# A kernel that plans its own instruction order: two prices of its planner and the size of four copies are changed

## The chip, the cores and the metric

The kernel runs on one core of one Trainium2 chip. The core has TensorE (PE in the profile, PEld for its weight loads), VectorE (DVE), ScalarE (ACT), GpSimd (POOL) and a queue for transfers (SP). The metric is the time of one execution on the device, in microseconds (us). Less is better.

## The reference

The reference runs three blocks over 256 tokens of width 1024, all in float32. It has six feed-forward networks around three token mixers: a short convolution, a gated delta rule, and a pair of sparse attention and an RWKV-7 scan. Cut to the part that matters here, the gated delta rule (16 value heads, 8 key heads of width 128) is:

```
a = strict_lower(einsum(k_beta, k) * decay)       # one key matrix per head and chunk
t_inv = solve(eye + a, eye)                       # its triangular inverse
u, w = t_inv @ v_beta, t_inv @ (k_beta * exp(g))
out = ... @ w_out                                 # after the state recurrence over chunks
```

Before it stands a projection `x @ w_in` that gives q, k, v, z and the gates, with a causal convolution of four taps over q, k and v.

## The kernel before

All weight matrices are cut into 128x128 tiles, four tiles to a chunk of 256 KB, and streamed from HBM in the order of use. A float32 product is made of three matmuls in the fast 32-bit format ("streamed products" below): each chunk `wraw` is split by ScalarE into `whi` (a copy) and by VectorE into `wlo` (the rest), the activations likewise into `xh` and `xl`, and TensorE multiplies whi by xh, whi by xl and wlo by xh, 256 columns each, into a bank of PSUM. Seven split chunks can be held ahead.

While the projection of the gated delta rule streams, the work of the mixer is done beside it: 256-column results are taken from the banks, the convolution taps of a v column (`conv`, three scalar_tensor_tensor on VectorE) read the bank itself, so the bank is free only when its last tap is done; from the eleventh column on, this product has three banks in turn, two columns to a bank (the line `banks=lambda g: 7 if g < 3 else 3`).

Beside it runs the chain `side`: the key matrices `TT` of 16 heads and two chunks of 128 tokens are inverted. `to_blocks` gathers their 32x32 diagonal blocks with copies on ScalarE and turns them with one VectorE transpose of 128x1024. `invert_blocks` then does 62 dependent VectorE instructions (31 steps of a product and a subtraction), `from_blocks` two more such transposes, and `inverse` goes from 32x32 to 128x128 by small matmuls. All that follows (values, states, outputs, and so the projection `gdn_out` behind it) waits for that inverse. The RWKV mixer later uses the same functions for 16 matrices.

The order of instructions on each engine is not that of the program text. Every instruction is recorded as a node with a price in us (`Pace.price`) and its dependences. `Pace.ranks` lays all nodes out by list scheduling over the five engines, forward and backward in five rounds (`Pace.schedule`), keeps the shortest plan, and `Pace.arrange` fixes each engine's order as the plan has it. So a price never changes how long an instruction takes; it changes the order in which engines take their instructions. An engine that is free in the plan takes the node of the highest priority that is ready. The chain `side` is put back by 3 us in priority (`SIDE = -3.0`). The prices also move the clocks by which the parts of the program are interwoven when it is written down (`weave`) and by which chunks are split ahead (`split_ahead`). The plan ends an instruction before it takes the next: a ScalarE copy holds ScalarE for its whole price.

Of the kernel before, what the change touches and what calls it, by code (L numbers as in the profile page):

```python
# [12 lines left out]
F32R = mybir.dt.float32r  # L13
U32 = mybir.dt.uint32
AF = mybir.ActivationFunctionType
# [244 lines left out]
class Pace:  # L260
# [43 lines left out]
    def price(self, engine, op, out, ins, kw):  # L304
        n = 1
        for d in (ins[0] if op == "tensor_reduce" else out).shape[1:]:
            n *= d
        if engine == "tensor":
            return self.columns(op, out, ins)[0] / 2400 + 0.0025
        held = 0.06 if hasattr(kw.get("scale"), "tensor") or hasattr(kw.get("bias"), "tensor") else 0.0  # L310
        bank = ins and self.parts(ins[0])[0][0].startswith("bank")
        if engine == "scalar":
            return (0.05 if bank else 0.09) + n * 0.00084 + 1.5 * held + (0.09 if "accum_out" in kw else 0.0)
        if engine == "gpsimd":
            return 0.1 + n * 0.002
        if op in ("tensor_copy", "tensor_scalar", "memset"):
            return 0.07 + n * (0.00104 if bank else 0.0006)
        if op == "reciprocal":
            return 0.07 + n * 0.00625
        return (0.13 if op == "scalar_tensor_tensor" else 0.07) + n * 0.00104  # L320

    def columns(self, op, out, ins):
# [42 lines left out]
    def schedule(self, order, before, after, forward):  # L365
# [16 lines left out]
        while left:  # L382
# [10 lines left out]
            else:  # L393
                t, e = min((free[e] if now[e] else max(free[e], later[e][0][0]), e) for e in free if now[e] or later[e])
                while later[e] and later[e][0][0] <= t:
                    _, o, i = heapq.heappop(later[e])
                    heapq.heappush(now[e], (o, i))
                o, i = now[e][0]
                _, price, _, cols = self.nodes[i]
                if e in self.LOOK and forward and later[e]:  # L400
                    w = min((c for c, u, j in later[e] if j in self.urgent and i not in self.urgent and c - t < self.WAIT * price), default=None)
                    if w is not None:
                        free[e] = max(w, t + 1e-6)
                        heapq.heappush(later[e], (free[e], *heapq.heappop(now[e])))
                        while now[e]:
                            heapq.heappush(later[e], (free[e], *heapq.heappop(now[e])))
                        continue
                if e == "tensor" and forward and len(now[e]) > 1 and cols[1] < 1500 * price:
                    while recent and recent[0][0] < t + price - self.TICK:
                        count -= recent.popleft()[1]  # L410
                    heavy = count + cols[1] < self.AIM + (self.MORE if heavy else 0)
                    if heavy:
                        o, i = min(((o, i) for o, i in now[e] if self.nodes[i][3][1] >= 2000 * self.nodes[i][1]), default=(o, i))
                        _, price, _, cols = self.nodes[i]
# [283 lines left out]
class Kernel:  # L698
# [769 lines left out]
    def to_blocks(self, TT, compact, blk):  # L1468

        M = TT.shape[1]  # L1470
        d = compact.rearrange("p (m i) -> p m i", i=32)
        for q in range(4):
            s = slice(32 * q, 32 * q + 32)
            self.nc.scalar.activation(d[s], TT[s, :, s], AF.Copy)
        d = d.rearrange("p m i -> p i m")
        if M == 16:
            d = d[:, :, None, :].to_broadcast([P, 32, 2, 16])
        self.nc.vector.transpose(blk.rearrange("p (j i) -> p i j", i=32), d)
# [745 lines left out]
```

## Time and profile before

| | |
|---|---|
| median of the runs shown | 1549.7 us (1548.59 to 1553.14, 3 runs) |
| the profiled execution | 1541.02 us |
| its span, first to last instruction | 1538.8 us |
| mean granted TensorE clock | 0.994 |

The profiled execution took 1541.02 us, of which 1538.8 us lie between its first and last instruction; 2.2 us lie around it. It is 0.56% below the median of the runs, so a change worked out in the profile is carried over by the ratio. Times in the trace count from the first instruction. All instructions are issued by one helper line, so the trace is read by tiles and not by lines.

### The profile page before, as it was taken

How to read it: one execution, taken by the hardware profiler on the slowest of the kernel's cores; microseconds unless marked ns; L12 is line 12 of the kernel's file. 1: busy time of each engine (PE TensorE's matmuls, PEld its weight loads, DVE VectorE, ACT ScalarE, POOL GpSimd, SP SyncE). 2: the span in 40 equal slices, each digit the busy share in tenths (PEclk: the TensorE clock that was granted, in tenths of full speed). 3: DMA queues.
4: the chain of work that ended last, by engine and by line, in shares of the span. 5: the costliest groups of instructions: out<-in, count | busy, mean ns of one | idle time of the engine just before them, and what ended most of it. 6: DMA issues, size and time to landing. Idle time of an engine off the chain costs nothing.

```text
span 1538.8 us, 35927 instructions
## 1 busy us (share of the span) xinstructions
PE 1522.6 (99%) x13544; PEld 1473.0 (96%) x13544; DVE 1197.5 (78%) x2527; ACT 1024.2 (67%) x2153; POOL 10.4 (1%) x24
## 2 busy tenths in 40 slices
PE   9999999999999999999999999999999999999999
PEld 9999999999999999989898899999997877999999
DVE  7776597887659777689997768775888866889984
ACT  7556566765657557678797866565783666578863
POOL 0000000000000000000000000000001000000000
PEclk9999999999999999999999999999999999999999
DMA  8766666566665667525343357666533313566674
GB/s 280 200 194 194 184 187 195 168 202 194 194 196 174 196 195 248 184 83 172 117 125 104 105 164 210 195 192 194 172 116 123 103 58 87 171 190 198 194 201 129
DMA packets 142670, 261.14 MB, mean 170 GB/s; under 512 B 15904, under 2 KB 17952, under 8 KB 142368
## 3 DMA queue, kind: packets, MB, share of 16 engines
q1 hardware_dynamic: 142496, 258.84, 56.8%
q8 instruction: 106, 1.74, 0.5%
q14 instruction: 68, 0.56, 0.1%
HBM read 257.73 MB, written 1.05 MB: 168 GB/s over the span
## 4 chain that ended last, share of the span: by engine, by line
PE 94%; DVE 3%; ACT 2%; issue 1%; DMA 0%; SPq 0%; DVEq 0%; ACTq 0%
PE bank L576 94%; DVE a L576 1%; DVE wlo L576 1%; ACT a L576 1%; DMA wraw<-wstream 0%; DVE arG L576 0%; ACT stm L576 0%; DVE stm L576 0%; ACT arG L576 0%; ACT whi L576 0%; DVE fg L576 0%; DVE xl L576 0%; DVE pad L576 0%; DVE tmp L576 0%; ACT pad L576 0%
## 5 line engine op out<-in xcount | busy, mean ns | idle before, releaser
L576 ACT ACTIVATE whi<-wraw 128x512 fp32r<-128x512 f32 x956 | 599.0, 630 | 398.7 <-PE bank L576 199.7
L576 DVE TENSOR_TENSOR wlo<-wraw,whi 128x512 fp32r<-128x512 f32 x956 | 652.4, 688 | 257.5 <-ACT whi L576 252.0
L576 PE MATMUL bank<-xh,whi 128*128 128x256 f32 x2688 | 745.4, 281 | 6.1 <-DVE stm L576 3.6
L576 PE MATMUL bank<-xh,wlo 128*128 128x256 f32 x2688 | 743.8, 281 | 0.0
L576 PE MATMUL bank<-xl,whi 128*128 128x256 f32 x2688 | 737.8, 279 | 0.7 <-DVE xl L576 0.7
L576 PEld LDWEIGHTS bank<-xh,whi 128*128 128x128 f32 x2688 | 503.0, 189 | 14.8 <-issue 5.6
L576 PEld LDWEIGHTS bank<-xl,whi 128*128 128x128 f32 x2688 | 501.4, 188 | 8.1 <-issue 6.2
L576 PEld LDWEIGHTS bank<-xh,wlo 128*128 128x128 f32 x2688 | 501.5, 188 | 6.6 <-issue 5.6
L576 PE MATMUL bank<-a,whi 128*128 128x256 f32 x2272 | 389.0, 277 | 0.3
L576 PEld LDWEIGHTS bank<-a,whi 128*128 128x128 f32 x2272 | 342.4, 188 | 1.3 <-DVE a L576 0.5
L576 PE MATMUL bank<-a,wlo 128*128 128x256 f32 x1136 | 313.8, 276 | 0.0
L576 PEld LDWEIGHTS bank<-a,wlo 128*128 128x128 f32 x1136 | 213.3, 188 | 0.0
L576 DVE TENSOR_TENSOR tmp<-bank,rb 128x256 f32<-128x256 f32 x176 | 66.2, 417 | 5.4 <-ACT rb L576 1.0
L576 ACT ACTIVATE xh<-h,par 128x256 fp32r<-128x256 f32 x70 | 34.1, 500 | 12.3 <-DVE h L576 10.8
L576 ACT ACTIVATE a<-tmp 128x256 fp32r<-128x256 f32 x88 | 35.6, 405 | 8.7 <-DVE tmp L576 8.7
L576 ACT ACTIVATE arG<-bank 128x256 f32<-128x256 f32 (+2 forms) x87 | 37.8, 443 | 4.9 <-PE bank L576 4.7
L576 DVE TENSOR_TENSOR acc<-acc,tmp 128x256 f32<-128x256 f32 x92 | 38.5, 418 | 2.0 <-ACT acc L576 0.9
L576 DVE SCALAR_TENSOR_TENSOR arG<-arG,par 128x256 f32<-128x256 f32 x88 | 40.0, 478 | 0.0
L576 DVE TENSOR_TENSOR a<-tmp,a 128x256 fp32r<-128x256 f32 x88 | 36.7, 417 | 3.8 <-ACT a L576 3.8
L576 PE MATMUL bank<-a 64*128 64x256 f32 (+3 forms) x192 | 38.1, 372 | 1.5 <-DVE arG L576 1.5
L576 ACT ACTIVATE tmp<-tmp 128x256 f32<-128x256 f32 x88 | 35.3, 406 | 3.8 <-DVE tmp L576 3.7
L576 DVE TENSOR_TENSOR tmp<-tmp,tmp 128x256 f32<-128x256 f32 x88 | 36.6, 416 | 0.0
(253 smaller groups left out, 1226.1 us busy)
## 6 DMA issues: line engine op xcount, KB each, us to landing
wraw<-wstream SPq DMA_DIRECT2D x968, 256.0 KB, 2.9
arG<-cmp_w SPq DMA_DIRECT2D x1, 1024.0 KB, 4.7
out_dram<-h SPq DMA_DIRECT2D x8, 128.0 KB, 3.0
con<-consts SPq DMA_DIRECT2D x1, 734.0 KB, 5.8
h<-xt SPq DMA_DIRECT2D x1, 512.0 KB, 6.3
a<-lowrank SPq DMA_DIRECT2D x1, 512.0 KB, 3.7
par<-params SPq DMA_DIRECT2D x1, 283.5 KB, 4.8
h<-xt SPq DMA_DIRECT2D x2, 128.0 KB, 3.6
```

What stands on the lines that cost most here:

```text
L576: i = f(*args, **kw)
```

## The change

Three edits. A streamed product of n columns is priced n/2259 us in place of n/2400 + 0.0025 (for 256 columns 113.3 ns in place of 109.2 ns). A VectorE transpose gets a price of its own, 0.07 + n x 0.00184 us in place of 0.07 + n x 0.00104 (for 1024 elements 1.95 us in place of 1.13 us). In `to_blocks`, each copy of diagonal blocks is done 16 matrices at a time: for the 32 matrices of the gated delta rule, eight copies of 32x512 elements in place of four of 32x1024; for the 16 of the RWKV mixer nothing changes.

```
-            return self.columns(op, out, ins)[0] / 2400 + 0.0025
+            n = self.columns(op, out, ins)[0]
+            return n / 2259 if ins[0].dtype == F32R else n / 2400 + 0.0025
...
-        if op == "reciprocal":
-            return 0.07 + n * 0.00625
+        if op in ("reciprocal", "transpose"):
+            return 0.07 + n * (0.00625 if op == "reciprocal" else 0.00184)
...
-            self.nc.scalar.activation(d[s], TT[s, :, s], AF.Copy)
+            for m in range(0, M, 16):
+                self.nc.scalar.activation(d[s, m:m + 16], TT[s, m:m + 16, s], AF.Copy)
```

## Rows read from the trace of the kernel before

**Rows 1.** The page: span, and each engine's busy time, share, instructions.

```profile
span 1538.8 us, 35927 instructions
...
PE 1522.6 (99%) x13544; PEld 1473.0 (96%) x13544; DVE 1197.5 (78%) x2527; ACT 1024.2 (67%) x2153; POOL 10.4 (1%) x24
```

**Rows 2.** Windows: stretch, length, busy us per engine, granted clock, DMA share, GB/s.

```profile
755.00:759.30 4.30, 4.30 (x40) 4.30 (x39) 2.56 (x6) 4.24 (x6) 0.00 (x0) 1.00 0.82 237
759.30:763.10 3.80, 0.22 (x2) 0.04 (x2) 3.80 (x10) 3.77 (x6) 0.00 (x0) 0.91 0.02 8
763.10:770.00 6.90, 6.89 (x31) 6.67 (x32) 5.99 (x18) 4.43 (x11) 0.00 (x0) 0.55 0.39 118
770.00:812.00 42.00, 41.78 (x426) 41.22 (x426) 39.97 (x104) 36.63 (x77) 0.00 (x0) 1.00 0.44 132
812.00:856.00 44.00, 42.16 (x582) 37.97 (x576) 29.35 (x59) 33.72 (x90) 0.00 (x0) 0.96 0.23 73
...
1100.00:1310.00 210.00, 205.99 (x1882) 171.23 (x1881) 167.89 (x401) 141.11 (x339) 9.08 (x18) 0.98 0.33 101
```

**Rows 3.** Waits from 750 to 775 us: who waited for whom, total, times, longest.

```profile
PEld bank L576 <- ACT acc L576: 3.8, 1, 3.8
...
DVE a L576 <- ACT a L576: 1.7, 1, 1.7
```

**Rows 4.** Timeline around that wait: start, length, engine, instruction, idle before it.

```profile
754.46 4.26 ACT L576 ACTIVATE a<-a 32x1024 f32<-32x1024 f32 x4
...
758.74 0.47 ACT L576 ACTIVATE tmp<-bank,par 128x256 f32<-128x256 f32 x1
758.75 2.12 DVE L576 STREAM_TRANSPOSE a<-a 128x1024 f32<-128x1024 f32 x1 [1.74 <-ACT a L576]
...
760.76 0.45 DVE L576 SCALAR_TENSOR_TENSOR tmp<-bank,par,tmp 128x255 f32<-128x255 f32 x1
...
762.09 0.87 DVE L576 SCALAR_TENSOR_TENSOR tmp<-bank,par,tmp 128x254 f32<-128x254 f32 x2
...
763.08 0.29 PEld L576 LDWEIGHTS bank<-xh,whi 128*128 128x128 f32 x1 [3.76 <-ACT acc L576]
```

**Rows 5.** Windows of a quiet streaming stretch, PE alone: busy us, matmuls, clock.

```profile
80.00:120.00 40.00, 40.00 (x355) 1.00 0.68 193
```

**Rows 6.** The page's DMA issues: the weight stream.

```profile
wraw<-wstream SPq DMA_DIRECT2D x968, 256.0 KB, 2.9
```

**Rows 7.** Groups by shape: count, busy us, mean ns, idle before.

```profile
L576 DVE STREAM_TRANSPOSE a<-a 128x1024 f32<-128x1024 f32 x6 | 12.6, 2116 | 4.4 <-ACT a L576 4.4
...
L576 ACT ACTIVATE a<-a 32x512 f32<-32x512 f32 x8 | 4.9, 626 | 0.1
L576 ACT ACTIVATE a<-a 32x1024 f32<-32x1024 f32 x4 | 4.2, 1055 | 0.0
```

**Rows 8.** Windows, only PE instructions that read xh: busy us, count, clock.

```profile
810.00:820.00 10.00, 3.98 (x16) 0.83 0.40 134
820.00:830.00 10.00, 3.11 (x18) 1.00 0.15 36
830.00:840.00 10.00, 2.27 (x9) 1.00 0.47 151
```

**Rows 9.** Timeline of VectorE: chunk splits and transposes back to back.

```profile
808.52 3.94 DVE L576 STREAM_TRANSPOSE a<-a 128x1024 f32<-128x1024 f32 x2
...
814.14 1.88 DVE L576 TENSOR_TENSOR wlo<-wraw,whi 128x512 fp32r<-128x512 f32 x3
```

**Rows 10.** Windows of ten us in the RWKV mixer, columns as in the second group.

```profile
1110.00:1120.00 10.00, 8.59 (x76) 8.40 (x75) 9.98 (x22) 8.60 (x18) 0.00 (x0) 1.00 0.75 242
...
1170.00:1180.00 10.00, 8.53 (x38) 6.14 (x38) 9.47 (x19) 1.22 (x3) 0.71 (x1) 0.83 0.17 52
...
1240.00:1250.00 10.00, 10.00 (x188) 8.08 (x189) 5.49 (x14) 9.08 (x21) 0.00 (x0) 0.83 0.39 129
```

## The prediction

> **What bounds the kernel now.** I read the page first. TensorE is busy for 1522.6 of 1538.8 us, no other engine for more than 78% [rows 1]. So only three things can change the time: the 16.2 us in which TensorE does nothing, the stretches in which its clock is low, and its work, which this change leaves alone. About 2 us of the idle time lie at the start and 3 at the end, which no order removes. Next the windows by stage: a quiet streaming stretch has no idle time at all [rows 5]; the idle time lies beside the two large mixers [rows 2]. Then the waits: the largest of TensorE in the gated delta rule is one of 3.8 us [rows 3]. The timeline shows where: at 763.08 us a weight load starts after 3.76 us of idling [rows 4]. Behind the wait the granted clock is 0.55 for 6.9 us [rows 2]. With only the levels 1.2 and 2.4 GHz, a mean of 0.55 is 90% of the stretch, 6.2 us, at 1.2 GHz, and half of that, 3.1 us, is lost. The place costs 3.8 + 3.1 = 6.9 us.
>
> What is late there? The waits name ScalarE's `acc`, but the load is the first of a new column, which needs a bank, and a bank is free when the last tap has read it: the two taps from 762.09 last 0.87 us and end at 762.96, 0.12 us ahead of the load [rows 4]. The taps are late because VectorE stood idle for 1.74 us for the block copies and then transposed for 2.12 us; ScalarE spent 4.26 us on four copies in a row, and the activation that starts the taps' column waited behind them until 758.74 [rows 4]. So this one wait lies just where all three edits act.
>
> **The change part by part.** No instruction's own duration changes but those of the copies. The rest is order.
>
> *Transposes.* Six, 2.12 us each in the mean, 1.97 back to back [rows 7, 9]. The price goes from 1.13 to 1.95, so the planner sees 0.82 us more for each and can put taps or splits first. Direct cost nothing.
>
> Here the Trainium skill speaks against the edit: its Vector Engine (DVE) Microarchitecture Reference, section "The reshape front-end and per-opcode configuration", says a transpose is pipelined to sustain one element per cycle per lane, an estimate of 1.07 us for 1024 elements at the 0.96 GHz that its page VectorE: DVE Perf Modes gives. By it the old price would be right and the edit worth nothing; the trace disagrees with twice that, 1.97 us.
>
> *Copies.* Four of 1055 ns become eight of 626 ns [rows 7]: 5.01 - 4.22 = 0.79 us more on ScalarE. It is busy in 36.63 of the 42 us from 770 on [rows 2], so this has room, but not in the 4.3 us ahead of the transpose, where ScalarE is 4.24 us busy [rows 2]. The gain is that ScalarE can take another instruction every 0.6 us instead of every 1.05: the tap's activation and two splits stood behind the copies. What is queued behind a copy on ScalarE is thus less delayed; what waits for all eight copies (the transpose, the chain) comes up to 0.79 us later, more if splits go between.
>
> *Streamed products.* 968 chunks of four tiles [rows 6] with three matmuls each are 11,616; each is planned 4.1 ns longer, 48 us in all. The quiet stretch gives 40 us / 355 = 112.7 ns [rows 5]; the old price is 3.2% short, the new 0.5% long. In the old plan TensorE needs its splits and banks earlier than it really does.
>
> The Trainium skill's page TensorE: Matmul & The Clock Gate, section "Wait — 56ns, not 53.3ns?", gives a warm matmul its columns over 2.4 GHz plus about 2.5 ns, an estimate of 109.2 ns: the old price to the digit. By that rule the edit would make the plan 48 us too long and place work too early on TensorE; by the row it removes an error of 3.5 ns a matmul. The row decides.
>
> What the new order is worth has no row. The bounds: *at the stall*, all of its 6.9 us can go, since 1.74 us of idling and a transpose of 2.12 us put off together are 3.86 us, over the 3.76 of the wait [rows 4]. But what becomes late next? The chain of the inverse. From 755 to 812 us VectorE works nearly without a gap: idle are 1.74, 0, 0.91 and 2.03 us [rows 2], 4.7 in all, and the chain's 62 instructions share it with taps and splits. Putting taps first puts the chain back by as much. From 812 on TensorE fills the chain's waits with what is left of the stream: 43 matmuls that read xh between 810 and 840 us [rows 8], with the one in three that reads xl 43 x 1.5 = 65, at 112.7 ns 7.3 us. If the stream arrives 6.9 us earlier, nearly all of this cover is used up before, and TensorE waits for the chain. So the lower end of the gain is what the chain itself gets earlier: 1.74 us of idling less 0.79 of longer copies = 0.95 us. The upper end is 6.9. Between them I take the middle, 3.9: VectorE's other idling gives the chain up to 2.9 us more, and some small matmuls of the chain do not need the cover.
>
> *Elsewhere* the order is drawn anew with no known sign. In the RWKV mixer TensorE idles 4.0 us [rows 2] and two stretches of ten us with a clock of 0.83 cost 1.7 us each [rows 10]: 7.4 us to win at most. One more wait like the present one costs 6.9. I take 0, with about 4 to either side. SP's and POOL's work is the same in number; loads follow the splits, and the stream's transfers land in 2.9 us with six buffers [rows 6], so they are not late unless splits are.
>
> Sum in the profiled execution: 1541.0 - 3.9 = 1537.1 us. That execution is 0.56% below the median shown, so 1549.7 x 1537.1 / 1541.0 = 1545.8 us; I say 1546.
>
> **The rivals.**
>
> *All of it is kept.* The chain is not what TensorE waits for after 812 us; 42.16 of 44 us are busy there now [rows 2], which speaks for it, the 7.3 us of cover against it. 6.9 us less, 1549.7 x (1541.0 - 6.9) / 1541.0 = 1542.8 us; with some of the mixer's 7.4, down to 1539.
>
> *Nothing is gained.* The planner puts a different wait in the place: taps come in time, but the chain's head is late by what they took, and TensorE idles just as long at 812 us with the same low clock after it. For it: VectorE is the scarce engine from 755 to 812. 1549.7 us, give or take 2.
>
> *Slower: two errors that cancelled.* VectorE's prices stay short. A split of 512 elements is priced 0.07 + 512 x 0.00104 = 0.60 us and takes 1.88 / 3 = 0.63 [rows 9]; a tap of 255 is priced 0.13 + 255 x 0.00104 = 0.40 and takes 0.87 / 2 = 0.435 [rows 4]: 4% and 10% short, beside TensorE's 3.2%. Until now the plan was fast on both sides alike; now it is right on TensorE alone and puts the chain's matmuls after too few streamed products. Over the 38 us from 770 to 808 that the chain's steps take, 4 to 10% is 1.5 to 3.8 us of waiting at the head of the inverse; the RWKV mixer has a like chain. Two waits of 2.5 us with 3.1 us of low clock behind each are 11; less the 3.9 won, +7: 1557 us. It decides from the point at which such waits pull the clock down: one of 1.4 us in the stretch from 1110 did not, one of 1.5 us from 1170 stands beside 0.83 [rows 10]. Against it: TensorE's waits are short today although the plan's balance is already imperfect.
>
> **How the numbers follow.** About 0.3%, 4.6 us, is what can be told from no change. Chances: my forecast (1 to 6 us gained) 0.40, all kept 0.21, nothing 0.21, slower 0.18. Of the forecast's spread two fifths lie beyond 4.6 us: faster 0.21 + 0.16 = 0.37; same 0.24 + 0.21 = 0.45; slower 0.18. The range from 1539 to 1554.5 leaves some 0.05 below (all kept and most of the RWKV mixer's gaps too) and 0.15 above (most of the slower case). The likeliest case alone: 1543 to 1549.
>
> **What would show it.** Right: in the profile after, the chain's ScalarE copies are eight of 0.63 us with splits or activations between them; no wait of TensorE over 2 us near 760 us and a granted clock of 1.00 there; the streamed product at 112.7 ns as before; between 812 and 856 us fewer matmuls that read xh, and more idle time than the present 1.8 us. Wrong: a wait of over 2 us with a clock of 0.6 behind it still there or at the head of the inverse (the second or third rival), or none anywhere and the span down by 7 us or more (the first). It would be wrong too if the order of the RWKV mixer moved the span by more than the gated delta rule does.

## The result, and the profile after

The changed kernel takes 1559.4 us in the median of 18 runs (1543.69 to 1572.28), the kernel before 1549.99 us in 18 (1541.07 to 1559.16): a ratio of 1.0058, 95% interval 1.0035 to 1.0081. (The ratio leaves out the one execution of 1572.28 us, over 1.5% above the fastest of its kernel.) Slower by 9.4 us, where 3.9 us were forecast as won. The profiled execution after took 1558.14 us; the one before, 1541.02 us, lay at the low end of its runs, so the two profiled executions lie 17.1 us apart (their spans 17.2), more than the medians.

The page of the kernel after, span and busy time [rows 1]:

```profile
span 1556.0 us, 35931 instructions
...
PE 1541.6 (99%) x13544; PEld 1488.3 (96%) x13544; DVE 1195.1 (77%) x2527; ACT 1026.1 (66%) x2157; POOL 10.5 (1%) x24
```

TensorE is busy for 19.0 us more with as many matmuls, and idles 1.8 us less. So the loss between these two profiles is no waiting: the same matmuls take longer. First the place that the prediction spoke of. The waits of the kernel after from 750 to 765 us [rows 3], and the timeline [rows 4]:

```profile
PEld bank L577 <- ACT acc L577: 1.6, 1, 1.6
PEld bank L577 <- DVE tmp L577: 1.5, 1, 1.5
...
DVE a L577 <- ACT a L577: 1.2, 1, 1.2
```

```profile
753.83 5.94 ACT L577 ACTIVATE a<-a 32x512 f32<-32x512 f32 x9
...
756.09 0.19 PEld L577 LDWEIGHTS bank<-xh,whi 128*128 128x128 f32 x1 [1.46 <-DVE tmp L577]
...
756.34 1.89 DVE L577 TENSOR_TENSOR wlo<-wraw,whi 128x512 fp32r<-128x512 f32 x3
...
759.81 2.17 DVE L577 STREAM_TRANSPOSE a<-a 128x1024 f32<-128x1024 f32 x1 [1.18 <-ACT a L577]
...
760.27 0.30 PEld L577 LDWEIGHTS bank<-acc,con 128*128 128x128 f32 x2 [1.61 <-ACT acc L577]
```

The one wait of 3.76 us has become two of 1.46 and 1.61 us. The eight small copies run in a row on ScalarE (the ninth of the row is a copy of 128x1024). VectorE puts taps and three splits ahead of the transpose, which comes at 759.81 in place of 758.75 us, and idles 1.18 us in place of 1.74. Then the windows by stage of the kernel after [rows 2]:

```profile
755.00:770.00 15.00, 12.50 (x103) 12.16 (x103) 13.82 (x34) 14.88 (x31) 0.00 (x0) 1.00 0.33 105
770.00:812.00 42.00, 41.35 (x445) 39.98 (x443) 41.99 (x113) 37.62 (x76) 0.00 (x0) 1.00 0.45 140
812.00:856.00 44.00, 43.40 (x483) 38.64 (x484) 22.49 (x41) 24.23 (x49) 0.00 (x0) 0.77 0.21 67
...
880.00:1100.00 220.00, 219.45 (x1858) 218.21 (x1858) 152.68 (x293) 133.62 (x264) 0.00 (x0) 1.00 0.63 187
```

The low clock behind the stall is gone: 1.00 where it was 0.55. It stands now in the inverse, 0.77 from 812 to 856 us: 20.5 us at 1.2 GHz from 821.8 on. And one loss has neither a wait nor a low clock. A quiet streaming stretch, windows of PE alone, first of the kernel after, then of before:

```profile
960.00:1000.00 40.00, 40.00 (x342) 1.00 0.62 186
```

```profile
960.00:1000.00 40.00, 40.00 (x355) 1.00 0.68 195
```

342 matmuls in place of 355 in 40 us, all busy, at a clock of 1.00. Taken singly, the matmuls start 117 or 118 ns apart (117.8 in the mean) in place of 113 or 114 (113.3), from 919 to 1126 us, but for gaps of 305 to 365 ns at the ends of products. I call this the slow rhythm.

So each execution with a profile is taken apart in three: the clock, half of the time at 1.2 GHz; the rhythm, 4.5 ns for each step of 116 to 119 ns between two streamed matmuls; and the rest, span less both, taken as what the order itself makes. For the first two profiles:

```
                 span    clock  rhythm  rest
before         1538.8      8.5     2.5  1527.8
changed        1556.0     13.7    11.8  1530.6
difference       17.2      5.2     9.3     2.8   (from unrounded values)
```

### The profile page after: what moved, and what is told of

The parts are those of the page before. It is cut to its first block, busy times and chain, and to the rows that moved or that the text cites. A ratio compares the mean times of both kernels' runs of the same rounds, so it can differ in the third digit from the quotient of the medians.

```text
span 1556.0 us, 35931 instructions
## 1 busy us (share of the span) xinstructions
PE 1541.6 (99%) x13544; PEld 1488.3 (96%) x13544; DVE 1195.1 (77%) x2527; ACT 1026.1 (66%) x2157; POOL 10.5 (1%) x24
## 3 DMA queue, kind: packets, MB, share of 16 engines
q8 instruction: 106, 1.74, 0.5%
## 4 chain that ended last, share of the span: by engine, by line
PE 92%; DVE 4%; ACT 2%; issue 1%; DMA 1%; SPq 0%; DVEq 0%; ACTq 0%
PE bank L577 92%; DVE a L577 1%; DVE arG L577 1%; DVE wlo L577 1%; DVE stm L577 1%; DMA wraw<-wstream 1%; ACT a L577 1%; DVE tmp L577 1%; ACT whi L577 0%; ACT stm L577 0%; ACT arG L577 0%; SPq L577 0%; DVE fg L577 0%; ACT arM L577 0%; ACT fg L577 0%
## 5 line engine op out<-in xcount | busy, mean ns | idle before, releaser
L577 PE MATMUL bank<-a,whi 128*128 128x256 f32 x2272 | 393.1, 278 | 0.5 <-DVE a L577 0.3
```

Source lines behind the costliest of these rows:

```text
L577: i = f(*args, **kw)
```

## The experiments

Theories: A, the streamed price is to blame; B, the transposes or the copies; C, executions differ by chance and the change does nothing; D, the order before is one of the better draws, and any new order is slower; E, two errors of the prices cancelled before (the third rival); F, later, the change's prices are worse than a small step would be. Ratios are to the kernel before on the same chip, with 95% intervals.

**e1, the streamed price alone.**

```
-            return self.columns(op, out, ins)[0] / 2400 + 0.0025
+            n = self.columns(op, out, ins)[0]
+            return n / 2259 if ins[0].dtype == F32R else n / 2400 + 0.0025
```

> Only the price of the streamed products is changed. Theory A (the new stream price puts the chain of the gated delta rule too close behind the stream and brings the low clock near 820 us): about 1.006 of before, 9 us more, and over 10 us at the low clock between 800 and 860 us in the profile. Theory B (transposes and copies carry the loss): 0.998 to 1.002. Theory C (no edit has a cost of its own; executions draw their low-clock stretches and their rhythm of the stream by chance): 0.997 to 1.003, and the profile less its low-clock loss and less its stretches at 117.8 ns a product comes within 3 us of before's.

**e2, transposes and copies; e3, the transposes alone; e4, the copies alone** (the diff's second and third edit, then each by itself).

```
+        if op in ("reciprocal", "transpose"):
+            return 0.07 + n * (0.00625 if op == "reciprocal" else 0.00184)
...
+            for m in range(0, M, 16):
+                self.nc.scalar.activation(d[s, m:m + 16], TT[s, m:m + 16, s], AF.Copy)
```

> The transposes' price and the eight copies, with the old stream price. Theory A: 0.996 to 1.001, the 3.8 us wait near 760 us gone or halved and no more low clock than before. Theory B: about 1.006. Theory C: 0.997 to 1.003.

> Only the price of the VectorE transposes. Theories A and C: 0.997 to 1.002; the wait near 760 us changes little, because the idle time ahead of the transpose comes from the copies. Theory B: 1.003 or more here or in the run with copies alone.

> Only the eight copies. Theories A and C: 0.997 to 1.002; the 1.74 us in which VectorE idles ahead of the transpose falls under 1.3 us. Theory B: 1.003 or more here or in the run with the transposes' price alone.

Measured: e1 1.0104 (1.0048 to 1.0160, 6 runs), e2 1.0091 (1.0054 to 1.0127), e3 1.0067 (1.0036 to 1.0098), e4 1.0023 (0.9992 to 1.0054). Each price alone costs as much as the whole or more; the parts do not add up, so neither A nor B stands alone. Of the signs, e1 has A's low clock (17.1 us at 1.2 GHz between 800 and 860 us). In e4 VectorE idles 0.76 us ahead of the transpose, as was expected. Two were missed: in e3 the longest wait of TensorE near 760 us fell to 1.5 us, where little change was expected, and in e2, where A had the wait gone or halved, a longer one came, 5.37 us for ScalarE's copy `arG` out of a bank, with a low clock:

```profile
761.54 0.29 PEld L576 LDWEIGHTS bank<-con,tmp 128*128 128x128 f32 x2 [5.37 <-ACT arG L576]
```

```profile
755.00:770.00 15.00, 8.38 (x38) 6.82 (x37) 12.92 (x32) 10.92 (x25) 0.00 (x0) 0.66 0.36 92
```

**e5 to e8: a small step up, one down, a step away from the truth, and the whole change with VectorE's prices raised too.** e5, e6 and e7 in this order:

```
-            return self.columns(op, out, ins)[0] / 2400 + 0.0025
+            return self.columns(op, out, ins)[0] / 2395 + 0.0025    (+0.2 ns)
+            return self.columns(op, out, ins)[0] / 2405 + 0.0025    (-0.2 ns)
+            return self.columns(op, out, ins)[0] / 2400             (-2.5 ns)
```

e8, on top of the whole change:

```
-        return (0.13 if op == "scalar_tensor_tensor" else 0.07) + n * 0.00104
+        return (0.17 if op == "scalar_tensor_tensor" else 0.095) + n * 0.00104
```

> The kernel before with its stream price longer by 0.2 ns only (256 columns: 109.4 ns in place of 109.2), which makes no price truer to speak of, but draws the order in the mixers anew. Theory D (before's order is a picked one, and any other draw of it is slower): 1.003 to 1.010, as the runs with single edits. Theory E (the price matters by its size; two errors cancelled before): 0.998 to 1.002. Theory C (chance of the executions): 0.997 to 1.003.

> The same in the other direction: 109.0 ns. Theory D: 1.003 to 1.010. Theories E and C: 0.997 to 1.003. If one of the two tiny changes is slow and the other is not, the order is a draw with a spread, and D stands only in part.

> The stream price moved away from the measured one: 106.7 ns for 256 columns. If a price nearer to the truth is worth something by itself, this is the slowest of the four, over 1.005. Theory D: 1.003 to 1.010, no worse than the tiny ones. Theory C: 0.997 to 1.003.

> The whole change, with VectorE's prices raised as well: the fixed part of a tensor_tensor from 0.07 to 0.095 us and of a scalar_tensor_tensor from 0.13 to 0.17, so that a split is priced 0.63 and a tap 0.435 us as the trace of before shows them. Theory E: 0.997 to 1.002, since both sides of the plan are now right. Theory D: 1.003 to 1.010, as the change.

Measured: e5 1.0033 (1.0004 to 1.0062), e6 0.9961 (0.9935 to 0.9986), e7 1.0033 (1.0002 to 1.0063), e8 1.0050 (1.0019 to 1.0080). E falls: with VectorE's prices raised as well, the change is as slow as without, within the intervals. A step of 0.2 ns, true to nothing, seems to move the time by 0.3 to 0.4%; for e6 this did not come back (e13, below).

**e9, e10 and e14: the kernels before and after, unchanged, profiled again.**

> The kernel before, unchanged, profiled once more. Theory C (the 117.8-ns rhythm and the 1.2 GHz stretches are drawn anew in each execution): the places change; some stretch of over 50 us at 117.8 ns or of over 10 us at 1.2 GHz can stand where the first profile had none, while the time without both stays within 1 us of 1527.8. Theory D (they come from the written order): the first profile again, 2.5 us lost to the rhythm, 8.5 us to the clock, each within 2 us and at the same places.

> The changed kernel, unchanged, profiled once more. Theory C: the 20.5 us at 1.2 GHz from 822 us or the slow rhythm from 919 to 1120 us, or both, are gone or elsewhere; the time without both is within 1 us of 1530.6, which leaves about 3 us to the order itself. Theory D: both stand where they stood, 13.7 and 11.8 us.

> The changed kernel, unchanged, a third profile. If rhythm and low clock are drawn in each execution: again other places or lengths than in the first (20.5 us at 1.2 GHz from 822 us; 117.8 ns from 919 to 1120 us) and the second (13.7 us from 1173 us; no long slow rhythm), with the time without both at 1530.6 to 1531.5 us. If they follow from the order and the second profile was the exception: the first one's places again.

Measured: spans of 1540.9 us (before), 1545.3 and 1546.1 us (changed, where the first profile had 1556.0). The windows of e10 at the two places where the first profile lost most:

```profile
812.00:856.00 44.00, 41.79 (x525) 36.42 (x526) 27.17 (x52) 31.65 (x86) 0.00 (x0) 1.00 0.22 67
880.00:1100.00 220.00, 219.84 (x1929) 219.39 (x1928) 157.03 (x308) 136.41 (x265) 0.00 (x0) 1.00 0.66 191
```

The same program: the clock in the inverse is 1.00 in place of 0.77, and 1929 matmuls stand where 1858 stood. In e10 the low clock stands at 1173 us instead, for 13.7 us. In e14 the slow rhythm lies near the start, windows of PE alone:

```profile
80.00:120.00 40.00, 40.00 (x342) 1.00 0.65 188
960.00:1000.00 40.00, 40.00 (x356) 1.00 0.68 195
```

So for the changed kernel theory C holds of the places: both losses are drawn in each execution. In the kernel before the low clock moves less: its second profile has the low clock at the same four places as the first and for as long, the third (e16) at nearly the same places, 10.2 us lost in place of 8.5.

**e11 and e12: the whole change with 256/2255 and 256/2263 us as the streamed price, 0.2 ns up and down.**

```
-            return n / 2259 if ins[0].dtype == F32R else n / 2400 + 0.0025
+            return n / 2255 if ins[0].dtype == F32R else n / 2400 + 0.0025    (e11; e12: 2263)
```

> The whole change with the streamed price 256/2255, 113.5 ns in place of 113.3. D (an order is a draw, and the kernel before is one of the better ones): the time moves by up to 0.4% to either side of the change's 1.0058, though no price has moved in truth; between 1.002 and 1.010. Theory F, a rival (the change's prices themselves are worth +0.6%, whatever the draw): within 0.1% of 1.0058.

> The whole change with the streamed price 256/2263, 113.1 ns. As for the other small step: D gives 1.002 to 1.010, and a difference between the two small steps of some 0.4%; F gives 1.0058 within 0.1% for both.

Measured: 1.0067 (1.0031 to 1.0104, 8 runs) and 1.0109 (1.0075 to 1.0142, 6 runs). F's first form, within 0.1% of 1.0058 for both, falls; but neither comes back to the small steps' level.

**e13 and e15 to e18: timed again** (the small step down, the change, the kernel before against itself, each price alone; code as above).

> The kernel before with its streamed price 0.2 ns shorter (256/2405), timed once more, since it was the best of eight draws and the best of several is flattered by chance. If its order is better in truth: 0.9961 again within 0.25%, with a mean clock loss of about 5 us against 10. If it was luck of the executions: between 0.999 and 1.001.

> The changed kernel, timed once more. If the order itself is slower: 1.002 (the 3 us that the time without slow rhythm and low clock is longer in three profiles against two) up to 1.006 again, and not 1.000. If the 1.0058 came from the executions of that day alone: 1.000 within 0.15%.

> The kernel before against itself: true ratio 1.0000. How far it comes out from that, beside its interval, is what two sets of executions of one program differ by; the two sets of the tiny step (0.9961, 1.0008) let me expect up to 0.25%.

> The streamed price alone, timed once more (1.0104 at first, from 6 executions). If changes of these prices make slower orders than steps of 0.2 ns do: over 1.005 again. If orders differ by chance alone and the sets of executions too: anywhere from 0.999 to 1.010.

> The price of the transposes alone, timed once more (1.0067 at first). If it is to blame for a good part: over 1.004 again, with a mean clock loss of some 16 us against 10. If not: below 1.003.

Measured: e13 1.0008 (0.9991 to 1.0025), e15 1.0061 (1.0034 to 1.0088), e16 1.0002 (0.9975 to 1.0029), e17 1.0062 (1.0030 to 1.0093), e18 1.0061 (1.0040 to 1.0083). The version that seemed to beat both kernels does not: 0.9961 did not come back. The change is slower again, and so is each price alone. So C falls as the cause of the slowdown. Of D the strong form falls: five timings of other orders (e4 to e7, e13) have a mean of 1.0012, ten of orders with one or both of the new prices lie between 1.0050 and 1.0109. Those orders are few, four and seven. And no step as large as the change's was made away from the truth, so whether the direction of a step or only its size costs time is not tested.

Single profiles, taken apart as above:

```
                              span    clock  rhythm  rest
before, again (e9)          1540.9      8.5     3.0  1529.4
before, third (e16)         1539.4     10.2     1.8  1527.3
changed, again (e10)        1545.3      8.5     5.3  1531.5
changed, third (e14)        1546.1      1.7    10.9  1533.4
changed, fourth (e15)       1543.6      6.8     3.7  1533.1
streamed price (e1)         1549.0     15.4     4.9  1528.7
streamed price (e17)        1545.6     13.7     4.1  1527.8
transposes' price (e18)     1552.5     18.8     3.3  1530.5
-0.2 ns (e6)                1536.6      5.1     2.8  1528.7
-0.2 ns, again (e13)        1552.2      5.1    16.2  1530.9
transposes and copies (e2)  1547.1      5.1     4.2  1537.8
eight copies (e4)           1557.9      8.5    16.1  1533.2
+0.2 ns (e5)                1550.5     17.1     3.2  1530.3
-2.5 ns (e7)                1543.7      9.0     2.9  1531.7
change, +0.2 ns (e11)       1542.8      0.0     3.2  1539.6
change, -0.2 ns (e12)       1564.0     10.8    19.7  1533.5
```

The rest is not free of the clock. Over the four profiles of the changed kernel, one order, it rises from 1530.6 to 1533.4 us as the clock's part falls from 13.7 to 1.7, and e11, with no low clock, has the largest rest of all. So half of the time at 1.2 GHz takes off somewhat too much, and differences of 1 to 3 us of rest do not weigh much.

And the timed executions, of which only span and mean granted clock are known, without a profile of each. The clock's part is span x (1 - clock); what remains holds order and rhythm together. Means:

```
                       executions  clock  remainder
before                        138   10.0     1533.7
changed                        29   13.0     1541.4
streamed price alone           17   15.1     1538.5
transposes' price alone        21   17.0     1536.9
eight copies alone             12    9.8     1539.7
-0.2 ns, first / again    12 / 12    5.1 / 5.0   1535.0 / 1538.8
+0.2 ns                        12   14.7     1536.3
```

These means go over several chips, and the kernel before itself lies between 1541.5 and 1545.8 us in span from one set with listed spans to another. Against the kernel before of its own set the change is 8.7 us slower in the mean at first and 10.0 us in e15.

The mean clock loss goes with the order (5.1 and 5.0 us in two sets of the small step), though a single execution can lie far from it (13.7 to 1.7 us in four profiles of the change). What parted the two sets of the small step lies in the remainder, and their profiles differ there by 13.4 us of rhythm. Against its own set's kernel before, this remainder is 0.4 us shorter in e6 and 7.5 us longer in e13, so the change's 7.8 us in e15 is no more than two sets of one order differ by.

**Where each price puts its low clock.** The streamed price alone (e17), windows of the inverse, and PE instructions that read xh [rows 8]:

```profile
812.00:821.00 9.00, 8.58 (x294) 7.82 (x289) 2.32 (x10) 8.74 (x16) 0.00 (x0) 0.98 0.02 5
821.00:833.00 12.00, 10.65 (x116) 9.41 (x114) 5.33 (x10) 11.48 (x20) 0.00 (x0) 0.50 0.15 44
833.00:836.00 3.00, 0.85 (x12) 0.66 (x10) 2.99 (x6) 0.00 (x0) 0.00 (x0) 0.50 0.90 264
```

```profile
810.00:820.00 10.00, 2.21 (x12) 1.00 0.01 3
820.00:830.00 10.00, 0.00 (x0) 0.53 0.09 29
830.00:840.00 10.00, 0.00 (x0) 0.50 0.43 131
```

12 matmuls read xh where 43 did [rows 8]: the stream that fills the chain's gaps is used up at 815 us. The clock falls at 821 us, while TensorE works on the chain's small matmuls, and the wait, 2.15 us, comes only at 833.5. e1 shows the same: 13.7 us from 821 and a wait of 2.3 us at 835. But so, in part, does the step of +0.2 ns: e5 has no matmul that reads xh from 830 to 840 us and 17.1 us at 1.2 GHz from 824 us:

```profile
755.00:770.00 15.00, 13.98 (x116) 13.50 (x114) 13.92 (x35) 13.05 (x23) 0.00 (x0) 1.00 0.41 121
770.00:812.00 42.00, 41.92 (x344) 40.75 (x345) 41.99 (x113) 39.13 (x81) 0.00 (x0) 1.00 0.52 153
812.00:856.00 44.00, 41.65 (x598) 37.28 (x598) 25.82 (x47) 26.20 (x58) 0.00 (x0) 0.81 0.19 56
```

The transposes' price alone (e18) has its largest low stretch in the RWKV mixer; below it the same stretch of the kernel before:

```profile
1250.00:1271.00 21.00, 21.00 (x199) 15.45 (x201) 8.89 (x23) 7.58 (x22) 0.00 (x0) 0.52 0.21 64
```

```profile
1250.00:1271.00 21.00, 21.00 (x320) 15.17 (x318) 13.05 (x35) 11.17 (x36) 0.00 (x0) 1.00 0.01 2
```

## Why the prediction was wrong

*The stall: it went, but not shown to be for the reason given.* The prediction said no wait over 2 us near 760 us and a clock of 1.00; all four profiles of the change have it so. To compare places I count the streamed matmuls, 11,724 in every kernel that is compared here. At the start of the 6500th (780 us) the four are ahead of the first profile of before, rhythm taken out, by 3.3, 4.4, 4.0 and 3.1 us, 3.7 in the mean: 3.4 of clock, and some of TensorE's idle time (3.59 us before, 1.22 and 1.41 after). That is half of the 6.9 us that could be won there. It is near the 3.9 us of the sum by chance, since those were to be what is left behind the chain of the inverse.

The edits need not be the reason. With the transposes' price and the copies (e2) the head of the chain did just what was forecast: tap activations ran between the copies, and VectorE idled 0.17 us ahead of the transpose. Yet TensorE waited 5.37 us, for another copy on ScalarE: that is the second rival's "different wait in the place". The streamed price alone (e1) has no wait over 0.7 us there. And the step of +0.2 ns, true to nothing, has none over 1.3 us and a clock of 1.00 (the windows of e5 above), and is 2.8 us ahead at 780 us.

*The copies: half right.* Their size was right, 623 ns for 626. Splits or activations between them on ScalarE there were none in the changed kernel; VectorE used the time instead.

*The streamed price: nearer to the truth than was thought.* 40 us / 355 counts matmuls that reach over the window's ends, so 112.7 ns is a little short. From start to start they are 113.3 ns apart, which is the new price.

*The transposes: their length right, their worth not.* They take 2116 ns again, 1.95 being the new price. By the Trainium skill (Vector Engine (DVE) Microarchitecture Reference, "The reshape front-end and per-opcode configuration"; an estimate of 1.07 us) the price would have moved away from the truth; by the trace it moved towards it, and alone it still costs 0.6% (e3, e18).

*The cover: not borne out for the whole change, right for the streamed price alone.* I expected fewer than 43 matmuls with xh from 810 to 840 us and more than 1.8 us of idle time from 812 to 856. The PE instructions of the kernel after that read xh [rows 8]:

```profile
810.00:820.00 10.00, 3.56 (x19) 1.00 0.41 133
820.00:830.00 10.00, 4.30 (x12) 0.59 0.21 61
830.00:840.00 10.00, 3.03 (x8) 0.50 0.14 49
```

That is 39, and 44 - 43.40 = 0.6 us of idle time (e10: 39 and 2.2). Neither is a sign: the window stands still while executions shift, and the kernel before has 43, 51 and 38 in its three profiles. The streamed price alone has 12 and 3.9 us: there the second rival, a late chain with idling and a low clock at the inverse, happened almost as written, but the clock fell ahead of the wait and not behind it. In the whole change the plan keeps the cover.

*Two terms of the sum failed.* One is "Between them I take the middle, 3.9", with 0.95 us as its lower end: of the gain at the stall nothing was kept. The other is "Elsewhere the order is drawn anew with no known sign ... I take 0". The runs showed +10.6 us in the mean of the timed executions (1554.4 for 1543.8, spans; 8.7 and 10.0 against the kernel before of the own set), in which the gain at the stall is already counted. By the parts, as estimates:

- Order: +4.0 us of rest (mean of four profiles 1532.2, of three before 1528.2; at an equal clock loss of 8.5 us, 1531.5 for 1527.8 and 1529.4). Most of it lies between the 6500th and the 6900th streamed matmul, from 780 to 880 us, in and behind the inverse: there the four profiles lose 1.4, 3.9, 4.5 and 3.8 us with clock and rhythm taken out, 3.4 in the mean. So the mixer ends no earlier: TensorE's wait at its end (0.8 us) is at 853.9 us in e10, and at 853.7, 855.7 and 851.4 in the three profiles of before. With only the rhythm taken out, at 880 us the four are 1.0 us behind the first profile of before in the mean (from 2.2 ahead to 6.6 behind). Other orders lose there too, that of the -0.2 ns step (e6, e13) 2.6 and 3.1 us, that of the -2.5 ns step (e7) 3.9, so this loss is not the change's alone. From the 9000th to the 9750th, in the RWKV mixer, the four lose another 1.3 us in the mean.
- Clock: +3.0 us in the timed executions (13.0 for 10.0). In the profiles it is 7.7 us for 9.1, the other way, so the sign is not sure; the step of +0.2 ns has 14.7 in the mean, that of -0.2 ns 5. What was won at the stall can be lost again in the inverse or in the RWKV mixer, not at one place: 20.5 us at 1.2 GHz from 822 us in the first profile, 13.7 from 1173 in the second, 3.4 in all in the third.
- Rhythm: the 3.7 us that remain of the 10.6, by difference. In the profiles it is 7.9 us for 2.4 (means of four and three). That it is drawn in each execution is shown; that the change makes it likelier is only seen in these means, and why would be open. The prediction has no term for it, since its one window of the stream showed a single rate [rows 5].

I knew from the trace that one more place like the stall costs 6.9 us, and set the mean of all such at 0. Whether the order before is a better draw than most is not shown: the small steps gave 0.9961 to 1.0033, with a mean of 1.0009 (e5, e6, e7, e13), the orders with a new price 1.0050 to 1.0109. That the change is slower was found twice (1.0058 and 1.0061). Why stays open. For the streamed price alone a part is seen: it uses up the cover (e1, e17). But the whole change has that price too and keeps the cover.

*The third rival* had the side and nearly the size (1557 us for 1559.4), but not the cause: raising VectorE's prices did not mend it (e8), and no wait of 2.5 us appeared in the changed kernel at the head of the inverse. *The first rival* did not happen. *The second rival* has its different wait in e2 and its late chain in e17, neither in the whole change; and both were slower, not level. The step by the median was sound: the profiled execution of before is a low one, as I had taken it.

## What to carry to other kernels

Where an order is planned from prices, a truer price is first of all another order: time it together with two or three steps of the same price that mean nothing, and once more the version that looks best, before the price gets the credit or the blame. Look in their profiles for the stall that the edit was made for: here a step of 0.2 ns removed it as well. Follow a gain at a stall to the end of the chain behind it; here 3.7 us at 780 us were gone at 880 in the mean of four profiles. Work that covers a chain's waits can be worth more than its own time: with a longer price of the stream the plan had spent it when the chain needed it (e1, e17).

## What the runs showed of the hardware

- The same streamed matmuls of 256 columns run at one of two steady steps, 113.3 or 117.8 ns, at a granted clock of 1.00. A rhythm can hold for long, some 180 us in e14 and 200 us in the first profile after, through gaps of 305 to 365 ns between products; where it sets in differs from execution to execution of one program. What chooses it stays open: at 919 us the first profile after started the product behind a gap of 148 ns and ran slow, before it was 142 ns and ran fast, but e14 ran fast behind a gap of 148 ns at 195 us. The 109.2 ns estimated from the Trainium skill (TensorE: Matmul & The Clock Gate, "Wait — 56ns, not 53.3ns?") is met by neither.
- The granted clock can stand at 1.2 GHz with TensorE busy all along, in one execution and not in the next. It fell at 821.8 us in the first profile after. Two windows of it, with all engines:

```profile
820.00:830.00 10.00, 10.00 (x136) 8.98 (x134) 3.43 (x6) 7.33 (x14) 0.00 (x0) 0.59 0.21 61
830.00:840.00 10.00, 10.00 (x76) 8.85 (x73) 4.35 (x8) 1.37 (x3) 0.00 (x0) 0.50 0.14 49
```

TensorE is not idle in either; e10, with the same order, has 1.00 in both.
- Single executions of one program spread by 1.2% (1541 to 1559 us, before) and 1.9% (1544 to 1572, after), and two sets of twelve differ by 0.5% (e6, e13). One profile of each kernel could not have shown what the change does: the first two differ by 17.2 us, later ones by 3 to 7.
